# Conditioning products by pairs of vectors on TensorE and by whole vectors on VectorE

## The chip, the cores and the metric

The kernel runs on one core of one Trainium2 chip. The metric is the time of one execution on the device in microseconds (us), the median of several runs. A profiled execution has its own time and, inside it, a span from the first to the last instruction.

## The reference

A trunk of two layers for 256 tokens of width 1024. What matters here is the conditioning: one vector `c` of 1024 values is put through SiLU and multiplied by a 1024 x 14336 matrix. The product falls into 14 vectors of 1024: shift, scale and gate for the mixer and for the expert part of each layer (vectors 0 to 11), and a shift and a scale for the keys and values (12 and 13).

```python
cond = jax.nn.silu(c) @ w_ada + b_ada
mods = cond[:, :n_layer_mod].reshape(B, DEPTH, 2, 3, D)
kv_mod = cond[:, n_layer_mod:].reshape(B, 2, D)
...
shift, scale, gate = mods[:, layer, 0, 0], mods[:, layer, 0, 1], 1.0 + mods[:, layer, 0, 2]
h = modulate(x, shift, scale)
y = mlstm_layer(h, ...)        # layer 0; layer 1 has attention
x = layer_norm(DEEPNORM_ALPHA * x + gate[:, None, :] * y, ln_g[layer, 0], ln_b[layer, 0])
...                            # then the same with 16 experts, two of them for each token
```

## The kernel before

The work runs in four stages: mixer A (mLSTM, 0 to about 310 us), the experts of layer 0 (to about 541 us), mixer B (attention, to about 690 us) and the experts of layer 1 (to the end). Every weight is read once from HBM, in pieces of 512 KB, by DMAs that SyncE (SP) issues in program order (`pieces`, line 209). The pieces stand in a ring of 20 slots of 128 x 1024 values; in the expert stages 18 slots more are added. The load of a piece waits until the piece that had its slot before has been used, so the loads run ahead of the engines by as much as the ring holds.

In the mixers a weight piece is split into a high and a low part (`split`, line 260: a copy on ScalarE, ACT, and a subtraction on VectorE, DVE), and TensorE (PE) then multiplies in three passes (`mm3`). `dense_cm` and `dense_tm` (lines 284 and 296) run these in blocks of 12 or of 6 matrix products of 256 or 512 columns, two blocks to a piece, and call `pump()` ahead of each block. `pump` (line 415) is what places the conditioning: each call adds a credit (`RATE`) to a purse and lets the generators in `todo` take steps for it; generators that only wait stand in `tail` and move one step per call.

Vectors 0 and 1 are made at the start and are not touched by the change. The other twelve are made by halves of 512 columns. A half loads four pieces with rows of 2 KB. Vectors 2, 4, 12, 6, 8 and 10 are made on PE (`ada_pe`, line 386): each of the eight rows-of-128 of a half is a product of 32 columns by 512, and the eight go to four groups of 32 columns of the array, two in each. So the four groups hold partial sums, and ACT copies them out. The other six vectors are made on DVE (`ada_steps`, line 368): eight multiply-adds of 128 x 512 into an accumulator, whose 128 partitions are partial sums. In both cases PE then adds over the partitions: for a shift or a scale by four products of a 128 x 128 block with one column (`ada_columns`, line 356), for a gate (2, 5, 8, 11) by two products that give a row (`ada_sum`, line 343). A product of fp32 values on PE is two instructions.

`before_moe` (line 469) ends each mixer: it finishes the vectors it needs (`ada_all`), builds the gate as a 128 x 1024 tile (`gate_rows`, line 439: two instructions on DVE that split the row, then six products on PE) and goes on. The compiler that orders each engine's instructions moves those of the conditioning as its own estimates of time tell it; they need not stand where `pump` was called.

Of the kernel before, what the change touches and what calls it, by code (L numbers as in the profile page):

```python
# [9 lines left out]
F32 = mybir.dt.float32  # L10
# [26 lines left out]
RATE = (0.9, 1.3, 0.9)  # L37
ON_PE = (2, 4, 12, 6, 8, 10)
# [119 lines left out]
def _body(ctx, tc, x, w_ada, a_w_in, a_wq, a_wk, a_wv, a_w_out, b_w_kv, b_wq, b_wo, moe_w_gate, moe_w_up,  # L158
# [68 lines left out]
    def piece(name, src):  # L227
        return pieces(name, src)[0]
# [108 lines left out]
    def is_gate(j):  # L337
        return j < 12 and j % 3 == 2

    def ada_load(j, hf, i):  # L340
        return piece(f"ada{j}_{hf}_{i}", w_ada[512 * i:512 * i + 512, D * j + 512 * hf:D * j + 512 * hf + 512])

    def ada_sum(j, hf, red, accs):

        ps = bankB(f"adaps{j}_{hf}")
        for z in range(2):
            o = ps[64 * hf + 32 * z:64 * hf + 32 * z + 32, 0:256]
            for q, a in enumerate(accs):
                T.matmul(o, red.to_broadcast([P, 32]), a[:, 256 * z:256 * z + 256], start=(q == 0), stop=(q == len(accs) - 1))
        if hf == 0 and j % 2 == 0:  # L350
            both = shared(f"mr{j}")
            gaterow[j], gaterow[j + 3] = both[:, 0:256], both[:, 256:512]
        q = slice(64 * hf, 64 * hf + 64)
        A.copy(gaterow[j][q, :], ps[q, 0:256])

    def ada_columns(j, hf, red, accs):

        pt = bankB(f"adat{j}_{hf}")
        for b in range(4):
            for q, a in enumerate(accs):  # L360
                T.matmul(pt[:, b:b + 1], a[:, P * b:P * b + P], red, start=(q == 0), stop=(q == len(accs) - 1))
        k = slice(4 * hf, 4 * hf + 4)
        V.tensor_tensor(mod[:, j, k], pt[:, 0:4], K("bada")[:, 8 * j + 4 * hf:8 * j + 4 * hf + 4], op=OP.add)

    def ada_end(j, hf, red, accs):
        (ada_sum if is_gate(j) else ada_columns)(j, hf, red, accs)

    def ada_steps(j, hf, nacc=1, delay=8):

        acc = [work[0].tile([P, 512], F32, tag="adacc", name=f"adacc{j}_{hf}_{i}") for i in range(nacc)]  # L370
        for i in range(2):
            w = ada_load(j, hf, i)
            for k in range(4):
                n = 4 * i + k
                c = csil[:, n:n + 1]
                a = acc[n % nacc]
                if n < nacc:
                    V.tensor_scalar(a, w[:, k, :], c, None, op0=OP.mult)
                else:
                    V.scalar_tensor_tensor(a, w[:, k, :], c, a, op0=OP.mult, op1=OP.add)  # L380
                yield 1
        for _ in range(delay):
            yield 0
        ada_end(j, hf, ones, acc)

    def ada_pe(j, hf, delay=2):

        ps = bankB(f"adapp{j}_{hf}")
        for i in range(2):
            w = ada_load(j, hf, i)  # L390
            for k in range(4):
                T.matmul(ps[32 * k:32 * k + 32, :], csil[:, 4 * i + k:4 * i + k + 1].to_broadcast([P, 32]), w[:, k, :],  # L392
                         start=(i == 0), stop=(i == 1))
        pr = work[0].tile([P, 512], F32, tag="adacc", name=f"adapr{j}_{hf}")
        A.copy(pr, ps)
        yield 8
        for _ in range(delay):
            yield 0
        ada_end(j, hf, C("sel4"), [pr])

    def run_all(g):
        for _ in g:
            pass

    todo = deque()
    tail = deque()
    rate = [1.0, 0.0]

    def step(g):
        try:  # L410
            return next(g)
# [1162 lines left out]
```

## Time and profile before

| | us |
|---|---|
| median of 3 runs | 932.9 (931.14 to 933.74) |
| the profiled execution | 932.29 |
| its span | 930.6 |
| PE busy in the span | 892.2 (96%) |
| DVE busy | 511.0 (55%) |
| ACT busy | 330.5 (36%) |
| DMA: share of its 16 engines | 91.8% |

Read it by stages: the shares of busy time are means over stages with different limits. A matrix product on PE is pipelined, so that its duration is longer than the distance from its start to the start of the next one. A view of PE that groups instructions gives busy time without counting overlaps twice.

### The profile page before, as it was taken

To read this page: it belongs to the slowest core of one execution; us is meant where nothing else is said; L and a number is where in the kernel's file an instruction comes from. 1 tells how busy PE (TensorE), PEld (TensorE's weight loads), DVE (VectorE), ACT (ScalarE), POOL (GpSimd) and SP (SyncE) were. 2 spreads that over 40 slices of the span, in tenths; PEclk is the share of its full clock that TensorE was granted. 3 is DMA by queue.
4 is the path that set the end of the run, shared out by engine and by line. 5 is a ranking of instruction groups with operands and counts; after the bars stand their busy time and mean duration, and the time that the engine had idled before them with its cause. 6 is when DMAs were issued, how large, how long until landed. Compare 5 with 4: busy or idle time off the path is not lost. (4 is left out here: it accounts for less than half of the span.)

```text
span 930.6 us, 13869 instructions
## 1 busy us (share of the span) xinstructions
PE 892.2 (96%) x5248; PEld 549.2 (59%) x5248; DVE 511.0 (55%) x984; ACT 330.5 (36%) x546; POOL 29.1 (3%) x41
## 2 busy tenths in 40 slices
PE   9999999999999899999999988999989999999985
PEld 5876988886788634344343467877764343434322
DVE  2475975866868824332332477967875323333317
ACT  3467665466554411111111046465552111111110
POOL 0020000000000000000000004020100000000000
PEclk9999999999999999999999999999999999999998
DMA  9999795697987989999999999776995999999992
GB/s 330 389 391 392 240 304 173 216 396 252 328 299 256 403 327 406 407 406 407 407 407 406 390 407 358 272 250 226 394 325 202 404 407 407 408 407 407 406 398 83
DMA packets 174210, 318.58 MB, mean 342 GB/s; under 512 B 10120, under 2 KB 28168, under 8 KB 174136
## 3 DMA queue, kind: packets, MB, share of 16 engines
q1 hardware_dynamic: 173992, 317.42, 91.8%
q8 instruction: 43, 0.70, 0.3%
q14 instruction: 31, 0.25, 0.1%
q10 hardware_dynamic: 144, 0.20, 0.1%
HBM read 316.53 MB, written 1.05 MB: 341 GB/s over the span
## 5 line engine op out<-in xcount | busy, mean ns | idle before, releaser
L135 PE MATMUL py<-w,aT 128*64 128x512 f32 (+1 forms) x576 | 118.2, 554 | 3.2 <-issue 2.2
L135 PE MATMUL pu<-w,xe 128*64 128x512 f32 x512 | 119.2, 596 | 0.5 <-DMA w<-in_moe_w_up_dram 0.4
L1231 DVE SCALAR_TENSOR_TENSOR yl<-py,wsl,yh 128x512 fp32r<-128x512 f32 x28 | 21.0, 750 | 176.0 <-ACT yh L1230 176.0
L135 PE MATMUL pg<-w,xe 128*64 128x512 f32 x512 | 116.1, 596 | 0.0
L135 PEld LDWEIGHTS py<-w,aT 128*64 128x64 f32 x576 | 41.3, 138 | 75.8 <-issue 65.1
L135 PEld LDWEIGHTS pu<-w,xe 128*64 128x64 f32 x512 | 36.3, 137 | 67.9 <-issue 60.8
L135 PEld LDWEIGHTS pg<-w,xe 128*64 128x64 f32 x512 | 34.8, 137 | 64.0 <-issue 58.9
L380 DVE SCALAR_TENSOR_TENSOR adacc<-ada,pk,adacc 128x512 f32<-128x512 f32 x84 | 61.9, 748 | 0.7
L1197 ACT COPY aT<-aT 128x512 f32<-128x512 f32 x16 | 9.4, 585 | 140.2 <-PE aT L135 140.2
L543 DVE TENSOR_TENSOR lntmpe<-po,gate 128x512 f32<-128x512 f32 x56 | 36.1, 684 | 38.6 <-PE po L135 38.6
L1230 ACT ACTIVATE yh<-py,wsl 128x512 fp32r<-128x512 f32 x28 | 19.2, 687 | 86.4 <-PE py L135 86.4
L521 ACT ACTIVATE xe<-ga,coef 128x256 f32<-128x256 f32 x32 | 16.1, 560 | 70.7 <-PE ga L135 70.7
L274 PE MATMUL z<-hh,wz 128*128 128x256 f32 x128 | 37.2, 291 | 0.0
L544 DVE TENSOR_TENSOR xt<-xt,lntmpe 128x512 f32<-128x512 f32 x56 | 36.0, 682 | 0.0
L275 PE MATMUL z<-hl,wz 128*128 128x256 f32 x128 | 36.0, 281 | 0.0
L276 PE MATMUL z<-hh,wz 128*128 128x256 f32 x128 | 35.9, 280 | 0.0
L1190 DVE TENSOR_TENSOR a<-a,pu 128x512 f32<-128x512 f32 x16 | 11.0, 689 | 37.0 <-PE pu L135 20.5
L392 PE MATMUL adapp<-ada,pk 128*32 128x512 f32 x192 | 30.8, 600 | 0.0
L135 PE MATMUL ga<-onehot,xh 128*128 128x256 f32 x128 | 30.7, 316 | 0.0
L135 PE MATMUL xm<-hh,win 128*128 128x256 f32 x144 | 28.8, 289 | 0.7 <-ACT hh L135 0.7
L1185 ACT ACTIVATE a<-pg 128x512 f32<-128x512 f32 x16 | 9.6, 597 | 52.2 <-PE pg L135 52.2
L135 PEld LDWEIGHTS ga<-onehot,xh 128*128 128x128 f32 x128 | 24.3, 213 | 5.9 <-DVE xt L544 4.1
(390 smaller groups left out, 1967.6 us busy)
## 6 DMA issues: line engine op xcount, KB each, us to landing
w<-in_moe_w_gate_dram SPq DMA_DIRECT2D x128, 512.0 KB, 10.2
w<-in_moe_w_up_dram SPq DMA_DIRECT2D x128, 512.0 KB, 10.2
w<-in_moe_w_down_dram SPq DMA_DIRECT2D x128, 512.0 KB, 10.2
ada<-in_w_ada_dram SPq DMA_DIRECT2D x112, 512.0 KB, 6.9
win<-in_a_w_in_dram SPq DMA_DIRECT2D x16, 512.0 KB, 8.5
wz<-in_a_w_in_dram SPq DMA_DIRECT2D x16, 512.0 KB, 6.4
wout<-in_a_w_out_dram SPq DMA_DIRECT2D x16, 512.0 KB, 8.2
wv<-in_a_wv_dram SPq DMA_DIRECT2D x8, 512.0 KB, 5.4
```

Source lines behind the costliest of these rows:

```text
L135: return self.tc.keep_in_program_order(f(*a, **kw))
L274: T.matmul(ps, l[0], r[0], start=start, stop=False, skip_group_check=True)
L275: T.matmul(ps, l[0], r[1], start=False, stop=False, skip_group_check=True)
L276: T.matmul(ps, l[1], r[0], start=False, stop=stop, skip_group_check=True)
L380: V.scalar_tensor_tensor(a, w[:, k, :], c, a, op0=OP.mult, op1=OP.add)
L392: T.matmul(ps[32 * k:32 * k + 32, :], csil[:, 4 * i + k:4 * i + k + 1].to_broadcast([P, 32]), w[:, k, :], start=(i == 0), stop=(i == 1))
L521: A.activation(dst, ps, AF.Identity, bias=sh[:, k:k + 1], scale=sc[:, k:k + 1])
L543: V.tensor_tensor(tmp, y, gate[:, c], op=OP.mult)
L544: V.tensor_tensor(dst[:, t, c], dst[:, t, c], tmp, op=OP.add)
L1190: V.tensor_tensor(a, a, pu, op=OP.mult)
L1230: A.activation(yh, py, AF.Copy, scale=wsl[:, b:b + 1])
L1231: V.scalar_tensor_tensor(yl, py, wsl[:, b:b + 1], yh.bitcast(F32), op0=OP.mult, op1=OP.subtract)
```

## The change

Six of the twelve vectors are still made on PE, now by pairs: (2, 5), (12, 13) and (8, 11). In a pair each of the four groups of 32 columns of the array holds one half of one vector and adds up all eight rows-of-128 itself (`ada_pair`), so that the sums are whole when they end; 32 products to a pair, in four steps of two rows-of-128, one step at each call of `pump`. One PSUM bank holds the pair for that time. A pair begins at a call of `pump` whose number is written out (`PAIRS`). For the gates, ACT and DVE write a high and a low part into one tile that `gate_rows` uses directly. Vectors 3, 4, 6, 7, 9 and 10 are made on DVE, now with one accumulator of 1024 columns; the credit for each call is about a third of what it was, and a step covers twice the columns. A vector starts only when the one before has left the accumulator. Its partitions are added by four products of 256 columns on PE into the four column groups. From these rows and from pair (12, 13) a copy on ACT and PE transposes (two or four) give the columns. Each load of a piece now takes a row-of-128 of a whole vector: 512 KB as before, with rows of 4 KB. Two buffers are renamed or moved, and two scratch pools lose a buffer.

```diff
--- before.py
+++ after.py
@@ -34,8 +34,8 @@
 RING = 10
 RING2 = 18
 EXTRA = 4
-RATE = (0.9, 1.3, 0.9)
-ON_PE = (2, 4, 12, 6, 8, 10)
+RATE = (0.25, 0.33, 0.33)
+PAIRS = ((2, 5, 8), (12, 13, 46)), ((8, 11, 20),)
 WA = 3
 WB = 3
 AHEAD = 100
@@ -334,77 +334,63 @@
         return keep.tile([P, 512], F32, tag="shared", name=name)
...
+    def ada_load(j, k):
+        return piece(f"ada{j}_{k}", w_ada[P * k:P * k + P, D * j:D * j + D])[:, 0, :]
+    def ada_columns(j, n, ps):
+        mr = small.tile([P, P * n], F32, tag=("cv" if n == 2 else "lntmp"), name=f"mr{j}")
+        A.copy(mr, ps)
+        yield 0
+        yield 0
+        pt = bankB(f"adat{j}")
+        for b in range(n):
+            T.transpose(pt[:, P * b:P * b + P], mr[:, P * b:P * b + P], ident)
+        o = slice(KD * j, KD * j + 4 * n)
+        V.tensor_tensor(mod.rearrange("p j k -> p (j k)")[:, o].rearrange("p (g b) -> p g b", g=4),
+                        pt[:, 0:P * n].rearrange("p (b g z) -> p g b z", b=n, g=4)[:, :, :, 0],
+                        K("bada")[:, o].rearrange("p (g b) -> p g b", g=4), op=OP.add)
+    def ada_vector(j, delay=3):
+        acc = work[0].tile([P, D], F32, tag="adacc", name=f"adacc{j}")
+        for k in range(KD):
+            w, c = ada_load(j, k), csil[:, k:k + 1]
+            if k == 0:
+                V.tensor_scalar(acc, w, c, None, op0=OP.mult)
+            else:
+                V.scalar_tensor_tensor(acc, w, c, acc, op0=OP.mult, op1=OP.add)
+            yield 1
         for _ in range(delay):
             yield 0
...
+        ps = bankB(f"adaps{j}")
+        for g in range(4):
+            T.matmul(ps[32 * g:32 * g + 32, 0:256], ones.to_broadcast([P, 32]), acc[:, 256 * g:256 * g + 256], start=True, stop=True)
+        busy.clear()
+        yield from ada_columns(j, 2, ps[:, 0:256])
+    def ada_pair(j, i):
+        ps = bankB(f"adapp{j}")
+        for k in range(KD):
+            w = [ada_load(v, k) for v in (j, i)]
+            for g in range(4):
+                T.matmul(ps[32 * g:32 * g + 32, :], csil[:, k:k + 1].to_broadcast([P, 32]), w[g // 2][:, 512 * (g % 2):512 * (g % 2) + 512],
+                         start=(k == 0), stop=(k == KD - 1))
+            if k % 2:
+                yield 0
+        if i == j + 1:
+            yield from ada_columns(j, 4, ps)
+        else:
+            hl = keep.tile([P, 512], F32R, tag="shared", name=f"mr{j}")
+            A.copy(hl, ps)
+            V.scalar_tensor_tensor(hl, hl.bitcast(F32), C("low"), ps, op0=OP.mult, op1=OP.add)
+            gaterow[j], gaterow[i] = (hl, 0), (hl, 2)
+    todo, tail, pairs, busy = deque(), deque(), deque(), []
     rate = [1.0, 0.0]
+    pumps = [0]
     def step(g):
         try:
@@ -417,39 +403,40 @@
         for p in list(tail):
             if step(p[1]) is None:
                 tail.remove(p)
-        rate[1] = min(rate[1] + rate[0], 4.0)
-        while todo and rate[1] >= 1:
+        while pairs and pairs[0][2] <= pumps[0]:
+            tail.append(pairs.popleft())
+        pumps[0] += 1
+        rate[1] = min(rate[1] + rate[0], 2.0)
+        while todo and rate[1] >= 1 and busy[:1] in ([], [todo[0][0]]):
             r = step(todo[0][1])
             if r:
+                busy[:] = [todo[0][0]]
                 rate[1] -= r
             else:
                 tail.append(todo.popleft())
     def ada_all(js=range(14)):
-        for q in (tail, todo):
-            for p in [p for p in q if p[0] in js]:
-                run_all(p[1])
+        for q in (tail, todo, pairs):
+            for p in [p for p in q if set(p[0]) & set(js)]:
+                for _ in p[1]:
+                    pass
                 q.remove(p)
-    def queue(js, r):
+    def queue(js, r, ps):
         rate[0] = r
-        todo.extend((j, (ada_pe if j in ON_PE else ada_steps)(j, hf)) for j in js for hf in range(2))
+        pumps[0] = 0
+        todo.extend(((j,), ada_vector(j)) for j in js)
+        pairs.extend(((j, i), ada_pair(j, i), n) for j, i, n in ps)
     def gate_rows(j):
         gt = keep.tile([P, D], F32, tag="gate", name=f"gate{j}")
-        parts = small.tile([P, 512], F32R, tag="lntmp", name=f"gp{j}")
-        hi, hl = parts[:, 0:256], parts[:, 256:512]
-        V.tensor_copy(hi, gaterow[j])
-        V.scalar_tensor_tensor(hl, hi.bitcast(F32), C("low"), gaterow[j], op0=OP.mult, op1=OP.add)
+        hl, g = gaterow[j]
         for h in range(2):
             pg = bankB(f"adag{j}_{h}")
-            r = 16 + 2 * (j // 3) + h
-            T.matmul(pg, pick[:, r:r + 1].to_broadcast([P, P]), lnr, start=True, stop=False, skip_group_check=True)
-            for g in range(2):
-                q = 24 + 2 * h + g
-                T.matmul(pg[:, 256 * g:256 * g + 256], pick[:, q:q + 1].to_broadcast([P, P]), hl, start=False, stop=(g == 1),
-                         skip_group_check=True)
+            for r, v in ((16 + 2 * (j // 3) + h, lnr), (24 + g + h, hl)):
+                T.matmul(pg, pick[:, r:r + 1].to_broadcast([P, P]), v, start=(v is lnr), stop=(v is hl))
             A.activation(gt[:, 512 * h:512 * h + 512], pg, AF.Identity, bias=ones)
         return gt
@@ -569,7 +556,7 @@
     actx = ExitStack()
     wsp = actx.enter_context(tc.tile_pool(name="wsp", bufs=WA))
-    work.append(actx.enter_context(tc.tile_pool(name="worka", bufs=2)))
+    work.append(actx.enter_context(tc.tile_pool(name="worka", bufs=1)))
     pa = actx.enter_context(tc.tile_pool(name="pa", bufs=1))
     pe = actx.enter_context(tc.tile_pool(name="pe", bufs=1))
     ph = pe.tile([P, KD, S], F32R, tag="hh", name="hh")
@@ -607,7 +594,7 @@
         w = wada[m, q]
         ps = bankB(f"adas{m}_{q}")
-        acc = [work[0].tile([P, 256], F32, tag="adacc", name=f"adacs{m}_{q}")]
+        acc = [pa.tile([P, 256], F32, tag="kq"[m], name=f"adacs{m}_{q}")]
         for k in range(KD):
             g = 32 * (k % 4)
             T.matmul(ps[g:g + 32, 0:256], csil[:, k:k + 1].to_broadcast([P, 32]), w[:, k, :],
@@ -820,7 +807,7 @@
     parts = xm_part(0, banks[0])
     for _ in start_dense(3, range(1, 3)):
         pass
-    queue((2, 3, 4, 5, 12, 13, 6, 7), RATE[0])
+    queue((3, 4, 6, 7), RATE[0], PAIRS[0])
     for h in range(1, NH):
         nxt = xm_part(h, banks[h] if h < 3 else None)
         qkv_part(h - 1, parts)
@@ -1388,7 +1375,8 @@
     wsp = bctx.enter_context(tc.tile_pool(name="wspb", bufs=WB, reuse_waits="tile"))
     pbh = bctx.enter_context(tc.tile_pool(name="pbh", bufs=1, reuse_waits="tile"))
     pb3 = bctx.enter_context(tc.tile_pool(name="pb3", bufs=3, reuse_waits="tile"))
-    work[0] = bctx.enter_context(tc.tile_pool(name="workb", bufs=2, reuse_waits="tile"))
+    work[0] = bctx.enter_context(tc.tile_pool(name="workb", bufs=1, reuse_waits="tile"))
+    pb2 = bctx.enter_context(tc.tile_pool(name="pb2", bufs=2, reuse_waits="tile"))
     pb = bctx.enter_context(tc.tile_pool(name="pb", bufs=1, reuse_waits="tile"))
     ptq = ctx.enter_context(ExitStack())
     pq = ptq.enter_context(tc.tile_pool(name="pq", bufs=1, side="right"))
@@ -1458,7 +1446,7 @@
             pt = bankB(f"bp{h}")
             for i in range(3):
                 T.transpose(pt[:, P * i:P * i + P], sb[:, par, P * i:P * i + P], ident)
-            pT.append(work[0].tile([P, 384], F32, tag="pT", name=f"bpT{h}"))
+            pT.append(pb2.tile([P, 384], F32, tag="pT", name=f"bpT{h}"))
             A.copy(pT[par], pt[:, 0:384])
         for t in range(NT):
             for par in range(2):
@@ -1469,7 +1457,7 @@
         V.tensor_tensor(ol_[:, e, :], po[:, 0:S], oh_[:, e, :].bitcast(F32), op=OP.subtract)
     with tc.issue_after(end.ins):
-        queue((8, 9, 10, 11), RATE[2])
+        queue((9, 10), RATE[2], PAIRS[1])
         k_part(0)
     modulated(xt, affine_split(qh, ql, scq, shq, "affq"), "tq")
     lnrow = pbh.tile([P, 2, D], F32, tag="oh", name="lnrow")
```

## Rows read from the trace of the kernel before

**Rows 1.** The page's 40 equal slices of the span.

```profile
PE   9999999999999899999999988999989999999985
DMA  9999795697987989999999999776995999999992
GB/s 330 389 391 392 240 304 173 216 396 252 328 299 256 403 327 406 407 406 407 407 407 406 390 407 358 272 250 226 394 325 202 404 407 407 408 407 407 406 398 83
```

**Rows 2.** Windows of 20 us: length, busy us (instructions) per engine, granted clock, DMA share, GB/s.

```profile
60.00:80.00 20.00, 19.70 (x120) 14.17 (x119) 18.32 (x31) 15.99 (x23) 0.22 (x2) 1.00 1.05 404
140.00:160.00 20.00, 20.00 (x144) 15.90 (x143) 11.40 (x14) 11.70 (x15) 0.30 (x1) 1.00 0.52 173
280.00:300.00 20.00, 20.00 (x102) 16.64 (x101) 17.08 (x34) 10.49 (x16) 0.00 (x0) 1.00 0.68 234
460.00:480.00 20.00, 20.00 (x108) 10.03 (x106) 8.49 (x17) 2.75 (x6) 0.00 (x0) 1.00 1.05 407
580.00:600.00 20.00, 17.57 (x124) 15.48 (x125) 19.24 (x25) 8.68 (x10) 1.29 (x1) 0.91 0.78 270
620.00:640.00 20.00, 19.80 (x153) 16.94 (x155) 11.90 (x21) 9.71 (x24) 1.28 (x4) 1.00 0.61 208
```

**Rows 3.** Waits, whole span: engine, line, released by: us in total, times, longest.

```profile
PEld pu L135 <- DMA w<-in_moe_w_up_dram: 4.7, 7, 1.1
PEld py L135 <- DMA w<-in_moe_w_down_dram: 3.2, 4, 1.6
```

**Rows 4.** Timeline of SP's queue where expert stages begin: start, us, loads issued.

```profile
312.53 4.81 SPq L224 DMA_DIRECT2D w<-in_moe_w_up_dram  x4
327.64 0.88 SPq L224 DMA_DIRECT2D w<-in_moe_w_up_dram  x2
...
689.64 0.93 SPq L224 DMA_DIRECT2D w<-in_moe_w_up_dram  x2
707.00 1.86 SPq L224 DMA_DIRECT2D w<-in_moe_w_up_dram  x2
```

**Rows 5.** Timeline of PE in mixer A, two products of 256 columns.

```profile
77.34 0.28 PE L275 MATMUL q<-cl,wq 128*128 128x256 f32 x1
77.45 0.28 PE L276 MATMUL q<-ch,wq 128*128 128x256 f32 x1
```

**Rows 6.** Groups by line and form: count, busy us, mean ns, idle before.

```profile
L392 PE MATMUL adapp<-ada,pk 128*32 128x512 f32 x192 | 30.8, 600 | 0.0
L361 PE MATMUL adat<-cs,adapr 128*128 128x1 f32 x64 | 7.9, 244 | 0.0
L361 PE MATMUL adat<-ones,adacc 128*128 128x1 f32 x64 | 7.9, 244 | 0.0
```

**Rows 7.** Timeline of PE: row sums of a gate's half.

```profile
88.09 0.28 PE L276 MATMUL k<-ch,wk 128*128 128x256 f32 x1
88.30 0.62 PE L349 MATMUL adaps<-adapr,cs 128*32 128x256 f32 x4
88.86 0.39 PE L274 MATMUL k<-ch,wk 128*128 128x256 f32 x1
```

**Rows 8.** Timeline of PE: halves in one block, in four, in a block of eight.

```profile
131.42 1.92 PE L392 MATMUL adapp<-ada,pk 128*32 128x512 f32 x16
133.28 0.38 PE L274 MATMUL q<-ch,wq 128*128 128x256 f32 x1
...
68.63 1.05 PE L392 MATMUL adapp<-ada,pk 128*32 128x512 f32 x4
69.61 0.50 PE L275 MATMUL v<-wv,mh 128*128 128x512 f32 x1
...
545.38 1.06 PE L392 MATMUL adapp<-ada,pk 128*32 128x512 f32 x8
```

**Rows 9.** Timeline of PE: eight instructions of 256 columns; transposes.

```profile
11.65 0.64 PE L135 MATMUL adas<-ada,pk 128*32 128x256 f32 x8
...
206.95 0.38 PE L912 MATMUL hnT<-cs,hn 128*128 128x128 f32 x2
...
37.46 0.63 PE L135 MATMUL tx<-cs,xt 128*128 128x128 f32 x4
```

**Rows 10.** Timeline of PE: the one-column sums of a half and their neighbours.

```profile
128.81 0.39 PE L276 MATMUL v<-wv,ml 128*128 128x512 f32 x1
129.04 0.95 PE L361 MATMUL adat<-ones,adacc 128*128 128x1 f32 x8
129.84 0.49 PE L274 MATMUL v<-wv,mh 128*128 128x512 f32 x1
```

**Rows 11.** Groups by line and form on DVE.

```profile
L380 DVE SCALAR_TENSOR_TENSOR adacc<-ada,pk,adacc 128x512 f32<-128x512 f32 x84 | 61.9, 748 | 0.7
L266 DVE TENSOR_TENSOR wz<-wz,wz 128x1024 fp32r<-128x1024 f32 x16 | 19.5, 1222 | 8.3 <-ACT wz L265 8.3
```

**Rows 12.** Timeline of mixer B: PE's waits, and DVE's operations around them.

```profile
576.58 0.39 PE L276 MATMUL bk<-kh,bk 128*128 128x256 f32 x1 [0.79 <-DVE bk L266]
582.43 0.39 PE L276 MATMUL bq<-qh,bq 128*128 128x256 f32 x1 [2.73 <-DVE bq L266]
...
573.00 0.48 DVE L378 TENSOR_SCALAR adacc<-ada,pk 128x512 f32<-128x512 f32 x1
579.45 2.93 DVE L266 TENSOR_TENSOR bq<-wq,bq 128x1024 fp32r<-128x1024 f32 x1
582.63 1.52 DVE L380 SCALAR_TENSOR_TENSOR adacc<-ada,pk,adacc 128x512 f32<-128x512 f32 x2
```

More of the change, by code (lines that the diff above doesn't have):

```diff
@@ L335, in shared @@
         return keep.tile([P, 512], F32, tag="shared", name=name)
[L337 to L381, printed above, removed]
+    def ada_load(j, k):
+        return piece(f"ada{j}_{k}", w_ada[P * k:P * k + P, D * j:D * j + D])[:, 0, :]
@@ L382, in ada_steps @@
+    def ada_vector(j, delay=3):
[7 more added lines that the diff above has]
+            yield 1
         for _ in range(delay):
             yield 0
[L384 to L406, printed above, removed]
+        ps = bankB(f"adaps{j}")
[19 more added lines that the diff above has]
+            gaterow[j], gaterow[i] = (hl, 0), (hl, 2)
```

## The prediction

> **What bounds the kernel now.** I read the page's slices first [rows 1]. PE is at 9 tenths nearly everywhere, and so is the DMA in the expert stages at 406 to 408 GB/s; in the mixers the DMA falls to 173 to 330. So the two may bound in turn, and the windows must tell which [rows 2]. In mixer A the DMA is busy for 0.52 of 140 to 160 us and 0.68 of 280 to 300 while PE is busy for 20.00 of 20 us: loads stand still because the ring is full, and PE sets the pace. In 460 to 480 the DMA moves 407 GB/s without a pause, and PE is busy for 20.00 too.
>
> Is a busy PE really working? That has to be asked, since its records overlap. Two products of 256 columns start 0.11 us apart though each lasts 0.28 [rows 5]: records end late, but starts follow each other closely. I followed the starts through mixer A; apart from a few gaps under 1 us the distances are those of an unhindered stream. So an instruction taken off PE there is worth its distance.
>
> Does such a gain reach the end? The expert stages end DMA-bound: PE waits for their pieces, 4.7 + 3.2 us in all [rows 3]. But the DMA stream that binds them is itself held back at their beginning: SP issues nothing between 317 and 327.64 us, nor between 690.5 and 707.00, since the ring is full [rows 4]. The slots come free when PE has gone through the mixer. A mixer that ends earlier moves the whole stream forward, one to one. So the sum is over PE's time in the mixers.
>
> **Part 1: PE time that goes.** Products for vectors on PE: 192 instructions, 30.8 us busy [rows 6]. Sums over partitions by one column: 64 + 64 instructions, 7.9 + 7.9 = 15.8 us [rows 6]; a check on the distance: eight of them stand between starts at 129.04 and 129.84, and the next start is late by 0.1, so 0.9 for eight, 14.4 for 16 halves [rows 10]. Row sums of the gates: eight halves at 0.62 = 5.0 us [rows 7]. Together 51.6 us, some 36 in mixer A (eight of the twelve vectors) and 16 in B.
>
> The Trainium skill (TensorEngine Tiling, section Instruction Overhead) says that each product carries some 60 cycles of overhead, so that one column costs as much as 60. By it, as an estimate, 128 one-column products at 2.4 GHz would be 3.2 us and not 15.8. The trace disagrees, 0.80 us between the starts for eight of them [rows 10].
>
> **Part 2: PE time that comes.** Three pairs of four steps; a step is eight products = 16 instructions of 512 columns over four column groups, the same number as an old half. An old half that ran in one block took 1.92 us, next start 1.86 after its own [rows 8]. Twelve steps: 12 x 1.92 = 23.0 us. Partition sums of six DVE vectors: eight instructions of 256 columns over four groups each; the start of the kernel has just that form at 0.64 [rows 9]: 6 x 0.64 = 3.8. Transposes: two for each of these six at 0.38, four for (12, 13) at 0.63 [rows 9]: 2.9. Together 29.7. Left over: 51.6 - 29.7 = 21.9 us.
>
> The 23.0 supposes that steps run in one block. In the old kernel halves often did not: 12 x 1.92 = 23.0 against 30.8 busy, 7.8 us too much. The cause is seen at 68.63: four instructions of one piece take 1.05 us, though eight take 1.06 and 16 take 1.92 [rows 8], because a piece of the old layout fed two column groups only, and other products were put in between. A new piece feeds two groups as well (half of the pair), so a step can fall into up to four parts. Bounds: none split, 0; all in four parts, 12 x (4 x 1.05 - 1.92) = 27.4 us. I take 5, somewhat under the old excess, because the twelve steps lie where the loads are ahead (part 4). Left: 17 us, about 12 in A and 5 in B.
>
> **Part 3: DVE.** An old operation of 512 columns takes 748 ns; 84 of them and 12 first ones. A new one of 1024 lies between 1.22 us (a two-operand operation of that width) and 2 x 0.748 = 1.50 [rows 11]; the step from 512 to 1024 columns of the first kind gives 1.29, which I take. DVE loses some 9 us over the kernel, and it is not the bound in most windows. One place is different. In mixer B PE waits 0.79 and 2.73 us for DVE at 576 to 582, DVE is busy for 19.24 of 580 to 600, and a split of 1024 columns takes 2.93 us there while the pool engine multiplies the residual [rows 2, 12]. The old kernel put its first conditioning operations there and behind (573.00, 582.63), after 18 calls of `pump`; with a credit of 0.33 the new one begins at the fourth call, so about three operations of 1024 come into the second key block. Queued behind each are the low parts of the splits that PE waits for. Price: 3 x 1.29 = 3.9 us; ends 0 (if they slip into gaps) and 3 x 2.93 = 8.8. I take 4. In mixer A DVE has room (11 to 18 of 20 us) [rows 2], price 0; where 60 to 80 is fullest, 18.32, two or three operations come in, but the first half made on PE leaves the same stretch.
>
> **Part 4: loads.** The number and size of the pieces stay (96 of 512 KB), rows go from 2 to 4 KB. At 2 KB the stream already moves 407 GB/s without pause [rows 2], and the conditioning is loaded mostly where the DMA has idle time, so I count 0. A pair asks for 16 pieces in four calls. At 407 GB/s that is 16 x 1.29 = 20.6 us of loading against 4 x (1.3 + 1.9) = 12.8 us of PE work (12 products at 0.11 [rows 5], and a step). The lack of 8 us, some six pieces, is covered by a ring of 20 that is full beforehand: before the first pair only eight pieces are used in its nine calls, before the second the DMA is busy at 0.52 [rows 2]. If that cover were gone, 8 us a pair, 24 in all.
>
> **Part 5: what is small.** Twenty copies on ACT become nine, the gate's split leaves the DVE queue ahead of the expert stages, `gate_rows` has four products in place of six: under 1 us on the path, counted 0. The bank that a pair holds leaves three to others; the third pair holds it while the first scores of attention want four: 0 to 2 us, counted 0.
>
> **Sum.** 17 - 4 = 13 us off the profiled execution's 932.3 (span 930.6 and 1.7 around it; the median of the runs is 0.6 above): 919 us.
>
> **Rivals.**
> - *The steps fall apart* (slower). All twelve run in four parts of 1.05 us: 27.4 in place of 5, so 932.3 - 13 + 22.4 = 942. For it: two vectors' pieces meet in each step, and six of the old halves were split in some way (the first at 68.63, the last at 545.38). Against it: the split in four happened once, while the DMA was saturated at 60 to 80 us [rows 2, 8]. It decides from about seven split steps (7 x 2.3 = 16 us) on.
> - *The expert stages are bound by their loads and give nothing back* (no change): 932. For it: PE does wait for pieces at their ends [rows 3]. Against it: the idle gaps of SP ahead of them [rows 4]. With it goes the case that PE only looks busy. The Trainium skill (Trainium Kernel Development and Optimization, section Performance Expectations) calls busy time of products a bad measure and weight loading a good one. By that, 15.90 of 20 us at 140 to 160 would leave PE a fifth of slack, and work taken off it would be worth less; the distances of the starts speak against that [rows 5].
> - *Waits eat most of it*: the three early DVE operations at 2.93 us, a pair's bank and the scratch buffers that the copies share with the mixers cost 8 to 9 us in place of 4, steps split as often as before: about 926.
> - *No split at all and no DVE price*: 932.3 - 21.9 = 910.
>
> **How the numbers follow.** The forecast, 919 (its own range 913 to 924): 0.52. About 926: 0.18. About 910: 0.12. No change: 0.08. Slower, 942: 0.10. A difference of 0.3%, 2.8 us, is what a measurement can tell. Faster 0.52 + 0.18 + 0.12 = 0.82, same 0.08, slower 0.10. The range takes in the first three with their edges: 907 to 930.
>
> **What would show it.** Part 1: no one-column products after 55 us. Part 2: `adapp` stays at 192 instructions with 23 to 28 us busy; above 35 the steps fell apart. Part 3: DVE operations of 1024 columns at about 1.29 us, and PE's waits for DVE in the second key block grow from 3.5 to about 7 us. Part 4: no waits of PE for `ada` pieces after the start; such waits of several us each would make the prediction wrong. The whole: the first loads of the experts after the gaps are issued some 12 us earlier than 327.64 and about 13 earlier than 707.00; if the first comes earlier and the end does not, the second rival is right.

## The result: slower by 8 us

| | before | after | ratio, 95% interval |
|---|---|---|---|
| median of the runs | 932.25 us | 940.25 us (939.79 to 941.05) | 1.008 (1.0064 to 1.0096) |
| profiled execution, span | 932.29, 930.6 | 940.66, 939.0 | |

The forecast was 919 us, and slower had a chance of one in ten. The page of the changed kernel, its 40 slices, against [rows 1] (`PEclk` is PE's granted clock in tenths of full speed):

```profile
PE   8999999998999799999999887999998999999995
PEclk9999999998999999999999998999998999999998
DMA  9999986499758979999999998997494999999993
GB/s 329 389 408 370 349 271 223 135 388 395 252 196 272 357 261 407 407 405 407 407 407 406 374 411 336 336 353 260 181 342 159 404 407 407 407 407 407 407 400 132
```

Before, PE had no slice below 9 ahead of 302 us. Now, besides the very first slice, there is an 8 at 211 to 235 us, with PE's clock below 9 tenths too, and the router's slice (302 to 329 us, just ahead of the experts), an 8 before, is a 7. In the windows of that stretch (columns as in [rows 2]) the kernel before has PE busy throughout at clock 1.00:

```profile
200.00:220.00 20.00, 20.00 (x105) 12.96 (x104) 12.04 (x34) 12.47 (x21) 0.00 (x0) 1.00 0.88 315
220.00:240.00 20.00, 20.00 (x139) 16.07 (x138) 16.24 (x26) 10.09 (x16) 0.00 (x0) 1.00 0.81 272
```

In the changed kernel it has gaps and a lower clock from 220 us on; the last two rows are mixer B's key and query blocks:

```profile
200.00:220.00 20.00, 20.00 (x141) 16.75 (x141) 13.34 (x29) 12.50 (x17) 0.00 (x0) 1.00 1.04 411
220.00:240.00 20.00, 15.63 (x58) 9.49 (x56) 16.30 (x29) 9.31 (x15) 0.00 (x0) 0.83 0.93 352
560.00:580.00 20.00, 17.44 (x139) 16.67 (x137) 19.93 (x19) 13.18 (x23) 10.65 (x4) 1.00 0.98 399
580.00:600.00 20.00, 17.60 (x126) 14.88 (x126) 11.28 (x13) 7.02 (x9) 0.13 (x1) 0.83 0.75 260
```

Where the time went is a table by landmarks of PE's timeline: the first `pg` (a product with an expert's gate weights, the start of an expert stage) and the first `tk` (a transpose, the start of mixer B). The kernel after was profiled a second time.

| profile | mixer A to `pg` | experts 1 | mixer B | experts 2 to end | span |
|---|---|---|---|---|---|
| before | 325.68 | 216.20 | 163.15 | 225.57 | 930.6 |
| after | 332.34 | 217.28 | 166.73 | 222.65 | 939.0 |
| after, second profile | 330.66 | 217.21 | 165.25 | 222.28 | 935.4 |

So mixer A lost 5.0 to 6.7 us where 12 were to be gained, mixer B 2.1 to 3.6 where one was. I split the mixers by PE's starts: a product's distance to the next start, less the idle time that the profile shows ahead of that one. Mixer A from 56 us on:

| us | before | after | difference |
|---|---|---|---|
| own work of the change (`adapp`, `adaps`, `adat`) | 33.04 | 23.94 | -9.10 |
| all other products | 231.63 | 235.79 | +4.16 |
| idle | 4.89 | 16.42 | +11.53 |

Mixer B has -3.78, +4.28 and +3.08. In the second profile the idle time is the same in both mixers within 0.3 us, and the other products are up by 2.3 and 2.9 only. The change took its own work off PE; waits, and slower products behind some of them, took more. The longest waits of PE in mixer A (56 to 332 us; what waits, what ended it: us in total, times, longest):

```profile
PE pp L1051 <- DVE mask L1045: 3.5, 1, 3.5
PE y L274 <- ACT av L270: 3.4, 1, 3.4
PE adat L348 <- ACT mr L343: 2.7, 2, 1.8
PE pgcol L789 <- DVE grow L781: 1.6, 1, 1.6
PE pr L980 <- ACT xT L976: 1.2, 1, 1.2
PE xm L275 <- DVE hl L135: 0.9, 1, 0.9
PE q L275 <- DVE cl L271: 0.8, 1, 0.8
```

The kernel before has the first of these (3.9 us), `xm` at 0.9, and else nothing above 0.4. The instructions of the change itself, against [rows 6, 11]:

```profile
L379 PE MATMUL adapp<-ada,pk 128*32 128x512 f32 x192 | 31.0, 599 | 0.0
L362 DVE SCALAR_TENSOR_TENSOR adacc<-ada,pk,adacc 128x1024 f32<-128x1024 f32 x42 | 57.9, 1379 | 0.2
L368 PE MATMUL adaps<-adacc,ones 128*32 128x256 f32 x48 | 5.0, 390 | 0.0
```

### The profile page after: what moved, and what is told of

Same layout as the page of the kernel before. It is cut to its first block, busy times and chain, and to the rows that moved or that the text cites. A ratio compares the mean times of both kernels' runs of the same rounds, so it can differ in the third digit from the quotient of the medians.

```text
span 939.0 us, 13576 instructions
## 1 busy us (share of the span) xinstructions
PE 886.2 (94%) x5141; PEld 541.1 (58%) x5144; DVE 503.3 (54%) x921; ACT 325.3 (35%) x535; POOL 29.4 (3%) x41
## 4 chain that ended last, share of the span: by engine, by line
PE 43%; DMA 8%; DVE 3%; ACT 1%; issue 0%; DVEq 0%; SPq 0%; ACTq 0%
PE py L135 8%; PE pg L135 8%; PE pu L135 7%; DMA w<-in_moe_w_up_dram 3%; PE po L135 3%; PE ga L135 3%; DMA w<-in_moe_w_down_dram 2%; DMA w<-in_moe_w_gate_dram 1%; PE bo L1454 1%; PE adapp L379 1%; DMA ada<-in_w_ada_dram 1%; PE bq L274 1%; PE bq L275 1%; PE bq L276 1%; PE s L1425 1%; PE by L274 1%
## 5 line engine op out<-in xcount | busy, mean ns | idle before, releaser
L362 DVE SCALAR_TENSOR_TENSOR adacc<-ada,pk,adacc 128x1024 f32<-128x1024 f32 x42 | 57.9, 1379 | 0.2
L135 PE MATMUL ga<-onehot,xh 128*128 128x256 f32 x128 | 30.8, 316 | 0.0
L274 PE MATMUL y<-wo,av 128*128 128x512 f32 x60 | 24.7, 414 | 3.4 <-ACT av L270 3.4
L135 PE MATMUL ga<-onehot,xl 128*128 128x256 f32 x128 | 27.7, 283 | 0.0
## 6 DMA issues: line engine op xcount, KB each, us to landing
w<-in_moe_w_gate_dram SPq DMA_DIRECT2D x128, 512.0 KB, 10.2
w<-in_moe_w_up_dram SPq DMA_DIRECT2D x128, 512.0 KB, 10.2
w<-in_moe_w_down_dram SPq DMA_DIRECT2D x128, 512.0 KB, 10.2
```

The source lines that it names most:

```text
L135: return self.tc.keep_in_program_order(f(*a, **kw))
L274: T.matmul(ps, l[0], r[0], start=start, stop=False, skip_group_check=True)
L362: V.scalar_tensor_tensor(acc, w, c, acc, op0=OP.mult, op1=OP.add)
```

## Where the largest new wait comes from

In an attention part PE makes `num` (scores times values), ACT and DVE turn it into `av` (transposed back on PE as `hnT`), and `y`, the output product, needs `av`. The timeline of PE in that stretch, before (36 products of `z` after the first `num` and the sums `adaps` are left out):

```profile
200.14 2.74 PE L877 MATMUL num<-v,sT 128*128 128x512 f32 x6
207.26 1.05 PE L392 MATMUL adapp<-ada,pk 128*32 128x512 f32 x2
208.23 0.87 PE L912 MATMUL hnT<-cs,hn 128*128 128x128 f32 x6
209.04 1.49 PE L392 MATMUL adapp<-ada,pk 128*32 128x512 f32 x11
211.30 2.84 PE L877 MATMUL num<-v,sT 128*128 128x512 f32 x6
214.03 0.50 PE L274 MATMUL y<-wo,av 128*128 128x512 f32 x1
```

and after, with the pair (12, 13) as a block of 64 at 173 to 183 us:

```profile
172.85 1.90 PE L379 MATMUL adapp<-ada,pk 128*32 128x512 f32 x10
174.96 6.19 PE L379 MATMUL adapp<-ada,pk 128*32 128x512 f32 x50
...
213.18 2.74 PE L864 MATMUL num<-v,sT 128*128 128x512 f32 x6
221.65 0.63 PE L368 MATMUL adaps<-adacc,ones 128*32 128x256 f32 x6
225.71 0.50 PE L274 MATMUL y<-wo,av 128*128 128x512 f32 x1 [3.43 <-ACT av L270]
227.39 0.69 PE L348 MATMUL adat<-cs,mr 128*128 128x128 f32 x2 [0.95 <-ACT mr L343]
227.87 5.33 PE L864 MATMUL num<-v,sT 128*128 128x512 f32 x6
232.21 1.42 PE L276 MATMUL y<-wo,axc 128*128 128x512 f32 x1
```

From the first `num` to `y` pass 13.9 us before and 12.5 after. A half of vector 12 (2.3 us from start to start) and the second `num` (2.73) stood there. Now neither does: the halves are gone, and the compiler has put the second `num` behind the first two `y`. PE stands still for 3.43 and 0.95, and the second `num` falls under a clock of 0.83 (mean of 220 to 240): its six take 4.34 us to the next start. This gave the **cover theory**: the old halves filled a stretch in which PE has to wait for ACT, and the pairs stand elsewhere. Rivals: **VectorE** (the 1.28 us operations make PE late) and **block** (64 products at once delay what the other engines wait for).

## The experiments

| kernel | median us | ratio to before, 95% | mixer A | mixer B |
|---|---|---|---|---|
| `half_before` | 916.8 | 0.982 (0.979 to 0.985) | 317.02 | 158.64 |
| `half_after` | 917.4 | 0.982 (0.980 to 0.985) | 318.84 | 159.32 |
| `late` | 931.2 | 0.998 (0.997 to 1.000) | 320.15 | 165.05 |
| `late_second` | 932.9 | 0.9995 (0.998 to 1.001) | 322.57 | 165.27 |
| `cover` | 928.1 | 0.994 (0.992 to 0.996) | 318.52 | 165.19 |
| `dve512` | 938.0 | 1.006 (1.004 to 1.008) | 325.83 | 165.79 |
| `no_dve` | 937.5 | 1.007 (1.004 to 1.010) | 331.69 | 159.23 |
| `b_vec` | 932.8 | 1.001 (0.999 to 1.003) | 333.10 | 159.19 |
| `vec_only` | 934.5 | 1.001 (0.999 to 1.002) | 328.77 | 162.43 |
| `pair_only` | 947.1 | 1.015 (1.013 to 1.017) | 338.10 | 171.85 |
| `late_b` | 925.8 | 0.990 (0.986 to 0.994) | 321.93 | 158.46 |
| `late_b_again` | 926.1 | 0.991 (0.989 to 0.993) | 323.35 | 159.86 |
| `late_b512` | 928.9 | 0.996 (0.995 to 0.998) | 322.34 | 160.31 |
| `late_ab512` | 928.8 | 0.9965 (0.994 to 0.999) | 325.19 | 160.14 |
| `cover_b` | 922.2 | 0.987 (0.984 to 0.990) | 317.64 | 158.43 |
| `after_again` (no edit) | 940.4 | 1.008 (1.006 to 1.010) | 330.66 | 165.25 |

**Is a product worth its distance?** Half of the products left out, in either kernel (the flags that mark the first and last product of a sum follow; not shown).

```diff
-            for k in range(4):                      # before, ada_pe
+            for k in range(4 if i == 0 else 0):
-            for g in range(4):                      # after, ada_pair
+            for g in range(4 if k < 4 else 0):
```

> The kernel before without the second half of its TensorE products for the pieces (the rows are loaded and the products of the second 512 rows left out, so those vectors hold half their sum). It leaves out some 96 of 192 products, half of the 28.7 us that they take of TensorE from start to start in the two mixers, so 14. Straight theory (each product is worth its distance, as predicted): 932.5 goes to 918 to 920. Gap theory (they stand in part where TensorE would wait anyway): 923 to 928.

> The changed kernel without the products of the second 512 rows of its pairs (the rows are loaded, the vectors hold half their sum): 96 of 192 products, half of the 28.7 us that they take from start to start, 14. If its pairs stand in full stretches, the whole of it comes back and more where waits follow them: 940 goes to 924 to 927. If they too stand in front of waits on the other engines: 930 to 934.

Measured: before falls by 16.9 us (14 by the straight theory; 3.6 of it stand in the last expert stage, of which below). In mixer A the distances of `adapp` fall by 9.8 and the stage by 8.7, idle grows by 0.9; in mixer B by 3.7 and 4.5. So in the old kernel a product thinned out was worth its distance, and the gap theory as I wrote it for this run is refuted: half of a filling still covers the wait for `av`.

The changed kernel falls by 23, over one and a half times what was left out. In mixer A the distances of `adapp` fall by 11.3, more than half of their 19.7, and the stage by 13.5, or 11.8 against the second profile. Its idle time stays the same within 0.2 us, though a block is now half as long. The wait for `av` is gone there, but not by any piece of the change: the compiler has put 47 products of `z` and the second `num` ahead of `y`, and other waits have come (up to 2.5 us for `wv`). So the order that the compiler chooses moves with every edit, and each comparison here contains it.

**Where the pairs stand.** An entry is a pair and the call of `pump` at which it begins (a step of the sequence, in the expectations).

```diff
-PAIRS = ((2, 5, 8), (12, 13, 46)), ((8, 11, 20),)
+PAIRS = ((12, 13, 68), (2, 5, 86)), ((8, 11, 20),)   # late
+PAIRS = ((2, 5, 8), (12, 13, 68)), ((8, 11, 20),)    # late_second
+PAIRS = ((12, 13, 46), (2, 5, 68)), ((8, 11, 20),)   # cover
```

> The changed kernel with the two vector pairs of mixer A at later steps of the sequence (12, 13 from step 68, 2, 5 from step 86), so that they stand between the attention parts and not among the dense products at 71 to 112 and 172 to 183 us. Gap theory: the old halves stood in stretches in which TensorE otherwise waits for ScalarE's and VectorE's chain, the new pairs stand in full ones; then the waits near 225 and 274 us (3.4, 1.0, 1.8 us) shrink, the clock does not fall there, and the time is 932 to 936. VectorE theory (the long 1024-column operations make TensorE wait): the place of the pairs matters little, 939 to 941. Starving theory (the first pair, in the middle of the first k products, makes the other engines late): the waits at 94 to 121 us go, some 2 us, 937 to 939.

> The changed kernel with only the second pair (12, 13) moved, from step 46 to step 68; the first pair (2, 5) stays at step 8. Splits the 9 us that the move of both gave. If the block of the second pair in front of the gates is what cost: 933 to 936. If the first pair among the first k products is what cost (VectorE then idles 12.5 us to 94 us): 938 to 940.

> The changed kernel with the pair (12, 13) left at step 46, where it runs as a block of 64 products at the gates, and the other pair (2, 5) moved from step 8 to step 68, between the first scores times values (num) and the first output products (y). Cover theory (what costs is that nothing is left to fill the wait for av between them): the waits of 3.4 and 0.9 us at 222 to 227 and the half clock behind them go, mixer A falls from 332 to 320 to 324, and the time to 928 to 933. Block theory (the block ahead of the gates itself makes the chain behind it late): mixer A stays at 328 to 332, the time at 936 to 940.

These moves alone give back 9.0, 7.4 and 12.2 us. `late` and `late_second` leave cover and block undecided, as both move the block. `cover` decides against block: the block of (12, 13) stays at the gates (`pgcol`), at 161 to 170 us, and only the other pair moves:

```profile
161.08 2.76 PE L379 MATMUL adapp<-ada,pk 128*32 128x512 f32 x18
164.43 5.35 PE L379 MATMUL adapp<-ada,pk 128*32 128x512 f32 x46
...
205.89 4.90 PE L379 MATMUL adapp<-ada,pk 128*32 128x512 f32 x41
211.66 0.44 PE L348 MATMUL adat<-cs,mr 128*128 128x128 f32 x2 [0.87 <-ACT mr L343]
213.71 2.74 PE L864 MATMUL num<-v,sT 128*128 128x512 f32 x6
216.38 1.92 PE L379 MATMUL adapp<-ada,pk 128*32 128x512 f32 x16
218.23 0.50 PE L274 MATMUL y<-wo,av 128*128 128x512 f32 x1
```

The wait for `av` is gone, the second `num` takes 2.67 us to the next start, the clock of 200 to 240 is 1.00, and the waits at 94 to 121 us that the pair at step 8 had brought (1.9 us together) are gone with it. The steps also stay together better: 128 products cost 15.98 us of distance in mixer A, 19.75 in the changed kernel, 20.15 before. Of the 14 us by which mixer A is shorter than in the changed kernel, 6.1 are idle time, 4.2 the change's own work, and 3.8 other products. The block theory falls. What the first pair's place among the first `k` products cost was the smaller part, 2.4 us (`late` against `late_second`), and that is the splitting of its own steps (`adapp` 16.2 us against 18.8), not starved engines: the idle time of the two is the same within 0.5 us.

The cover theory is borne out for the place, but one rival in it stays open: the compiler's order. In all seven profiles with more than 1 us of waiting for `av` here (`after` twice, `b_vec`, `no_dve`, `dve512`, `vec_only`, `late_ab512`) `y` stands ahead of the second `num`, in all others behind it. In `vec_only` a half stands in the stretch as before, but `y` comes first, and PE waits 1.88 us: so the order alone can leave about half of the wait. No run changes the order by itself.

**VectorE.**

```diff
             if k == 0: ...
-            else:                                   # no_dve: steps 1 to 6 left out
+            elif k == 7:
                 V.scalar_tensor_tensor(acc, w, c, acc, ...)
-        queue((9, 10), RATE[2], PAIRS[1])           # b_vec
+        queue((9, 10), 0.5, PAIRS[1]); rate[1] = -8.0
-                V.scalar_tensor_tensor(acc, w, ...) # dve512
+            for h in range(2): ... acc[:, 512*h:512*h+512] ...
```

> The changed kernel with only the first and the last of the eight VectorE steps of each vector (36 of 48 steps left out, all rows loaded, the vectors hold a quarter of their sum). Measures the whole price of the VectorE steps. As forecast (nothing in mixer A, 4 us in mixer B): mixer A stays at 276 us and mixer B falls from 166.7 to 163. Wait theory: A loses 3 to 6 us too, and B 5 to 8, 926 to 932 in all.

> The changed kernel with only the VectorE vectors of mixer B moved: they begin at about step 18, a step every second step of the sequence. Mixer A as it is. If the two placements are independent: mixer B falls from 166.7 to 158 to 160 us, 933 to 935 in all. If the expert stage or the start of mixer B takes it back: 937 to 940.

> The changed kernel with each VectorE step as two 512-column operations in a row, the same columns in all. VectorE theory: waits behind an operation of 1.28 us become waits behind one of about 0.75, TensorE's waits for VectorE shrink by a third, 936 to 938. Gap theory: no gain, and the added fixed cost of 48 operations is hidden or costs a little, 940 to 942.

Without three quarters of the steps mixer A is 0.65 us shorter (nothing: the second profile of the changed kernel is 1.0 shorter still), mixer B 7.5 (6.0 against the second profile). The median falls by 2.8 only; in the profile the last expert stage is 3.4 us longer than in the changed kernel's. `b_vec` keeps all of the steps, moves most of them out of the two key blocks (before the last split of `bk` there are two, at 563.26 and 566.05, in place of six), and mixer B gets the same: 159.19. So the price in mixer B is one of place too. DVE in the second key block of the changed kernel, against [rows 12], and PE's wait there:

```profile
563.85 1.28 DVE L362 SCALAR_TENSOR_TENSOR adacc<-ada,pk,adacc 128x1024 f32<-128x1024 f32 x1
569.37 3.46 DVE L362 SCALAR_TENSOR_TENSOR adacc<-ada,pk,adacc 128x1024 f32<-128x1024 f32 x1
572.76 5.17 DVE L271 TENSOR_TENSOR ql<-affq,qh 128x256 fp32r<-128x256 f32 x2
577.85 3.36 DVE L362 SCALAR_TENSOR_TENSOR adacc<-ada,pk,adacc 128x1024 f32<-128x1024 f32 x1
581.13 1.21 DVE L266 TENSOR_TENSOR bk<-wk,bk 128x1024 fp32r<-128x1024 f32 x1
582.40 0.58 PE L276 MATMUL bk<-kh,bk 128*128 128x256 f32 x1 [4.92 <-DVE bk L266]
```

The last `bk` that PE waits for stands behind a step of 3.36 us; in `b_vec` the wait is 3.03, in `no_dve` 0.62. The shorter wait is 1.9 us of what `b_vec` gains; most of the rest is other products, 3.2 to 4.4 us, where PE's clock is at its lower level for 10.2 us of mixer B against 12.7 and 17.1 in the two profiles of the changed kernel. `dve512` gained 6.5 us in mixer A (4.8 against the second profile), which the load of VectorE can't explain, since `no_dve` gained none there. It is not the wait for `av` either, which stays (3.56): the waits for `grow` (1.6), for the second `mr` (1.8) and for `kT` (0.8) are gone. Why the split takes those away is open. On top of a good placement the split gave nothing (`late_b512`, below).

**One half of the change at a time.**

```diff
+ON_PE = (2, 5, 12, 13, 8, 11)                        # vec_only: these by halves, as before,
+    for j in js: ... [ada_pe(j, 0), ada_pe(j, 1)] if j in ON_PE else [ada_vector(j)]
+    todo.extend(((j,), ada_steps(j, hf)) ...)       # pair_only: halves of 512 on VectorE
```

> The changed kernel's VectorE half alone: whole vectors on VectorE with column sums and transposes, its 4 KB rows, but the six TensorE vectors by halves spread over the sequence as in the kernel before, with their one-column sums. Gap theory: close to the kernel before, 930 to 934, since the halves are back in the gaps and half of the one-column sums are gone. VectorE theory: the loss stays, 937 to 942.

> The changed kernel's pairs alone: pairs on TensorE at the same steps as in the changed kernel, and the VectorE vectors by halves of 512 columns with one-column sums as in the kernel before. Gap theory: the loss stays and the one-column sums of the four VectorE vectors come on top (64 more products a mixer at some 0.06 us), 940 to 945. VectorE theory: 932 to 936.

The credits and the order of the vectors were set to match (not shown). Whole vectors with the old spread of halves: no change against before. Pairs with the old VectorE part: 15 us slower, more than expected. So pairs at those steps carry the loss, though there by other waits (for `av` 0.51 us, for `wv` 2.48 and 1.80, for `hn` 1.86) and by steps split still more (`adapp` 23.0 us in mixer A). The whole vectors with their transposes are worth 6.8 us beside them (`pair_only` against after); the one-column sums that they spare cost `pair_only` 7.2 us of distance in mixer A.

**Put together.** `late_b` is `late` with `b_vec`'s queue line, `late_b512` has `dve512`'s split too, `late_ab512` also a later first VectorE step in mixer A (rate 0.28 from -1.5), `cover_b` is `cover` with `b_vec`'s line.

> The kernel with both pairs of mixer A late, and in mixer B the two VectorE vectors begin at about step 18 and go a step every second step of the sequence, so that none of the 1.28 us operations stands in the two key blocks. VectorE theory for mixer B: the wait of 5.0 us for bk at 570 shrinks to the 1 to 3.5 of the kernel before, and with it two or three us: 928 to 929. Else the wait stays, since the weights are multiplied late for another reason (the other shared work of that stretch): 931 to 933.

> Both pairs of mixer A late, the VectorE vectors of mixer B late, and each VectorE step as two 512-column operations. If the long operation still makes others late: some 2 us more than without the split, 923 to 924. If the placement has already taken those waits away: 925 to 927, or a little more for 48 added operations.

> As the run before it, with the first VectorE step of mixer A some five steps of the sequence later, so that it is not ahead of cl, for which TensorE waits 1.8 us at 72. If that wait is the step's: 1 to 3 us gained, also the half clock behind it, 921 to 924. If cl is late for another reason: no change, 925.

> The changed kernel once more, with a new profile. If the length of the last expert stage (222.7 us here, 225.6 in the kernel before) belongs to the kernel, it is 222 to 223 again; if it is an accident of one execution, it may be 225 to 227.

> The fastest kernel so far once more (both pairs of mixer A late, the VectorE vectors of mixer B late), for a closer interval and a second profile: 924 to 927. If the length of its last expert stage (226.4 us) is its own, it is 226 to 227 again; if not, 222 to 223.

> The two cheapest placements together: in mixer A the pair (12, 13) at step 46 and the pair (2, 5) at step 68, in mixer B the VectorE vectors from about step 18. If they are independent, mixer A ends near 318.5 as in the run with the pair moved alone, mixer B takes 158 to 160 us in place of 165, and the time is 921 to 924. If one takes the other's gain: 926 to 928.

`late_b` came out better than expected, 926 in both runs. The split of the VectorE steps brought no gain, 929 in `late_b512` and `late_ab512`; for the second no more than 925 was expected. In `late_ab512` the wait for `cl` fell from 1.23 to 0.56, but the late pair slipped behind `y`, and the wait for `av` was back (3.56 us at 203.70), with `y` ahead of the second `num` again. `cover_b` has both placements changed and is the fastest, 11.6 us below the kernel before and some 18 below the changed one. Not all waits are gone with them: PE is idle for 19.1 us in its two mixers, 28.2 in the changed kernel and 13.3 before.

**Left open.** The last expert stage took 222 to 223 us in some profiles and 225.6 to 228 in others. Most of the difference stands ahead of the last `aT`, a wait put down to PE's sequencer; the two rows are of the changed kernel and of `late` (and the clock falls behind the longer wait):

```profile
PE aT L135 <- DVEq L1319: 1.3, 1, 1.3
...
PE aT L135 <- PEq L1319: 4.7, 1, 4.7
```

Two profiles each of the changed kernel (222.65, 222.28) and of `late_b` (226.39, 228.00) agree, yet the runs of one kernel lie in clusters some 5 us apart (`late_b`: 920.1, 920.4, and 925.8 to 927.6; `cover_b`: 915.4, 917.8, and 921.9 to 923.8, with its one profile, 222.8 us, from the lower cluster). Whether the stage's length belongs to a kernel or to an execution is not settled. By it the changed kernel's loss of 8 could be anything from 8 to 11 in like conditions, as its two mixers and first stage have it in the two profiles.

## Why the prediction was wrong, point by point

- **What bounds.** That PE sets the pace of the old mixers and that a product taken off is worth its distance held (`half_before`). The failed step stands here: I carried that sentence over to products that are moved. It holds as long as the work left in each stretch covers the chain of the other engines; I followed the starts of the old kernel, in which everything was covered, and did not ask which products did the covering. The sum has no term for where the added work stands. Measured: 14.6 us more idle time in both mixers, and 5.2 to 8.4 us more for products that the change does not touch, against 12.9 us of own work saved.
- **That a mixer's gain reaches the end** held nearly one to one for the first expert stage (216.2 to 218.2 us in all profiles but `vec_only`'s, 220.5); SP's first load after the full ring came at 334.30 in the changed kernel, 6.7 later than in [rows 4], as mixer A was 6.7 later:

```profile
314.87 3.10 SPq L224 DMA_DIRECT2D w<-in_moe_w_down_dram  x3
334.30 0.88 SPq L224 DMA_DIRECT2D w<-in_moe_w_up_dram  x2
```

- **Part 1** was too large: 51.6 us of busy time are 47.6 by distances, since the 30.8 of `adapp` are 28.7 and the 15.8 of the one-column sums 13.7. **Part 2** was right in total: 29.7 + 5 forecast, 34.7 by distances (`adapp` 28.7, sums 4.4, transposes 1.6). The steps did split, as much as the old halves; only in `late` and `cover` the 128 of mixer A cost 16. Own work saved: 12.9, not 17.
- **Part 3** had the place and the mechanism, and mixer A's price of 0 (0.65 measured, `no_dve`); the 4 us in mixer B measured 6.0 to 7.5, within its upper end of 8.8. PE's longest wait for DVE there grew to 4.9 us where about 7 were to be seen. The operation took 1.28 us (1.29 forecast), but 3.46 and 3.36 where POOL works, which I had kept for the end of the range only.
- **Parts 4 and 5**: after the start no product of the change waited over 0.3 us for a piece. The copy `mr` ahead of the transposes was counted among the small things; PE waited 2.7 us for it, where nothing covered it.
- **Rivals.** Waits eat most of it was the nearest, but its waits were those of DVE in mixer B and of banks; the largest was ACT's chain in mixer A. The steps fall apart gave almost the measured time, 942, for another reason: its sign of recognition, `adapp` above 35 us busy, did not come (31.0).
- **That PE only looks busy.** Half of the pieces' products left out of the old kernel were 13.5 us of distance and worth 13.2 in its two mixers (`half_before`), so PE had no slack there. The Trainium skill (Trainium Kernel Development and Optimization, section Performance Expectations) calls weight loading (beside MFU), and not the busy time of products, a good measure of how close a kernel is to roofline, its limit. By that, as the prediction read it, PE would have had a fifth to spare at 140 to 160 us [rows 2]; the run disagrees.

With both placements changed (`cover_b`) the mixers are 12.8 us shorter than before (8.0 and 4.7; forecast 12 and 1) and the median is 922.2 against the forecast of 919. The 12.8 are 17.9 us of own work saved (forecast 17) and 0.7 saved on other products, less 5.8 of added idle time: the sum of the work was about right, its place was not in it. That the added idle time comes near the 4 that were taken off for VectorE is luck, since 5.3 of it stand in mixer A, where none was expected.

## What to carry to other kernels

An engine without idle time may be so only because other work happens to lie in the gaps of another engine's chain. Before such work is merged into blocks or moved, list the chains that run beside it (here `num` to `y`, 12 to 14 us) and what fills each of them now, and leave a piece in each. Look at the order in the trace, too, since the compiler may move a filler that the edit did not touch (here the second `num`). And try the place first: here moving one pair changed the time by 12 us (`cover`), about as much as the change saves in work.

## What was not expected of the hardware

- A short wait can cost twice, and need not. Behind the two waits of 0.8 us at 70.7 and 73.4 us in the changed kernel, PE's granted clock was 0.69 as the mean of 71 to 76.5 us, and products of 256 columns started 0.21 us apart from 73.8 to 76.1 us, not 0.12: the lower of the two levels, 1.2 GHz. In the second profile of the same kernel the same two waits stand at 71.0 and 73.6 us, the clock stayed at 1.00, and the products stood 0.12 us apart. The first row is of the first profile, the second of the second:

```profile
71.00:76.50 5.50, 4.59 (x24) 3.44 (x24) 5.50 (x7) 4.99 (x9) 0.00 (x0) 0.69 1.03 409
71.00:76.50 5.50, 4.59 (x34) 3.36 (x35) 5.46 (x8) 5.21 (x9) 0.00 (x0) 1.00 1.03 410
```

  Over mixer A the clock is at its lower level for 13.7 us in the first profile and for 6.8 in the second; the idle time is the same, and the products that the change does not touch take 1.7 us longer in the first.

- One and the same VectorE operation, 1024 columns, took 1.28 us at 563.85 and 3.46 at 569.37. POOL had begun its two-operand work 0.02 us before the second:

```profile
569.35 5.75 POOL L553 TENSOR_TENSOR xt<-xt,lnrow 128x1024 f32<-128x1024 f32 x2 [409.95 <-ACT lnrow L478]
575.06 5.07 POOL L554 TENSOR_TENSOR xt<-xt,lnrow 128x1024 f32<-128x1024 f32 x2
```

The added 2.2 us are somewhat less than one of these POOL operations (5.75 / 2 = 2.9). The Trainium skill (SBUF — State Buffer, section SBUF: two separate sides) says that a VectorE operation with two SBUF operands and a GpSimd one that reads SBUF lock the port pair they share for a whole instruction, and that the other waits. The trace agrees in kind. From the two measured steps, an operation of this form is to be priced at 3.4 us in that stretch, not at 1.3.
